# Full-array broadcasts and head sums, and alternating column halves, in the mixer of a hybrid decoder trunk

## The chip, the cores and the metric

The kernel runs on one core of a Trainium2 chip. The metric is device time in microseconds (us); a time before or after is the median of several runs. Beside it one execution is profiled: every instruction has a start and a duration on its engine. PE is TensorE's matmul, PEld its weight load, DVE is VectorE, ACT ScalarE, POOL GpSimd, SP the queue that issues most transfers.

## The reference

Two decoder layers over a sequence of 512 tokens, model width 1024, all in float32. Only the mixer of layer 0 is touched by the change. Its lines, shortened:

```python
hn = rms_norm(h, mix_norm_w[0])
proj = hn @ hyb_w_in[0]                     # [z | xBC | dt | q | k | v]
# A: state space heads, 16 heads of 64, chunks of 128 tokens, state 128
a_cs = cumsum(dt * a_head)                  # per chunk
y_diag = (C B^T * exp(segsum(a))) (x dt)
y_off  = C (carried states) * exp(a_cs)
y_a = gated_group_rms_norm(y_diag + y_off + x * D, z, norm_w)
# B: 16 query heads of 64 on 2 key heads, window of 128 tokens, blocks of 128
q, k = rms_norm(q, q_norm_w), rms_norm(k, k_norm_w)      # over each head's 64 channels
p = softmax with sink (q k^T / 8 + bias, previous and current block)
y_b = p v
h = h + concat(y_a, y_b) @ hyb_w_out[0]
```

After it come a gated MLP, a convolution module and a second gated MLP, which the change leaves alone.

## The kernel before

Activations lie with channels on the 128 partitions and the 512 tokens along the row. A weight matrix is cut into tiles of 128x1024 that SP loads one after the other; `wsplit` cuts each into a high and a low fp32r part (ACT, then DVE), and `gemm` (L131) makes three matmuls of 512 columns for each of the eight inner tiles, at L136, L137 and L138. So one output tile of a projection is 24 matmuls. Products that are not split (transposes, L489, L506, L513, L681) are float32, and the trace has two matmul records for each of them.

The mixer runs through its head pairs j = 0 to 7 (heads j and j + 8 together). The loop at L558 puts out, for each j, a projection tile of x, a tile for queries or keys, and the stages of earlier head pairs: `ssd_states` (L461: transposes L465, two broadcasts L474), `ssd_carry` (L485: L489), `ssd_outputs` (L500: L506, the broadcast of `pair_bcast` at L259, L513). `head_sums` (L524) sums the squares of one query tile over each head for the norm. Then comes attention, `attn_prep` (L619, one `pair_bcast` for each head pair), `attn_logits` (L634) and `attn_values` (L662), in units of (head pair, block of 128 queries), the values three units behind the logits; the gate tiles (L704) are mixed in between. The order on each engine comes from the tile framework's scheduler at build time, outside the stretches of `manual_schedule`; on the chip each engine works through its list in order.

Four kinds of matmul are named below.

- Broadcasts. `rows_t` holds per-head rows (a value and its rounding rest, 32 rows each): partitions 64 to 127 the cumulated decays, partitions 0 to 63 the norm factors of queries and keys. A matmul with a selecting matrix spreads one row over the partitions: L474 for one head, L259 for the two heads of a pair. Both use 64 rows of the array and all 128 columns.
- Head sums at L533, with a selecting matrix of 32 columns, written to 32 partitions of `st_q`; the high part `cv` first, then the low part `th`.
- L506, the product within a chunk: 64 columns for head e = 0 go to partitions 0 to 63 of the bank, those for e = 1 to partitions 64 to 127. Four chunks c for e = 0, then four for e = 1. The operand `ms[0]` comes from DVE and `ms[1]` from POOL (L481).
- L681, the attention values, in the same two column halves: for e = 0 both key blocks b, then for e = 1.

Of the kernel before, what the change touches and what calls it, by code (L numbers as in the profile page):

```python
# [8 lines left out]
F32R = mybir.dt.float32r  # L9
# [5 lines left out]
P = 128  # L15
T = 512
NB = T // P
# [26 lines left out]

CONSTS = {}
_n = 0
for _name, _w in (("ident", P), ("triu", P), ("pairs", 18), ("halves", 73), ("stack", 32)):
    CONSTS[_name] = (_n, _w)
    _n += _w
NCST = _n  # L50
# [10 lines left out]
def kernel(ctx: ExitStack, tc: tile.TileContext, x, w_in, w_dt, w_out,  # L61
                             pw1, pw2, w_up0, w_up1, w_dn0, w_dn1, par, cst, btab, out):
    nc = tc.nc
    V, S, G, TE = nc.vector, nc.scalar, nc.gpsimd, nc.tensor
# [9 lines left out]
    def nm(s):  # L74
        uid[0] += 1
        return f"{s}_{uid[0]}"

    base = {"wr", "wh", "wl", "xr", "nsum", "nsq", "nvar", "nr", "nrb", "cv", "ct", "th"}
    phase = [sb]
# [10 lines left out]
    f32 = lambda ap: ap.bitcast(F32)  # L90
# [11 lines left out]
    def con(name):  # L102
        o, w = CONSTS[name]
        return ctile[:, o : o + w]
# [6 lines left out]
    ident, triu = con("ident"), con("triu")  # L111
# [113 lines left out]
    def mixer(norm, nxt):  # L225
# [21 lines left out]
        def hi_lo_rows(bank, r0):  # L247
            S.copy(rows_t[r0 : r0 + 64], bank[r0 : r0 + 64])
            V.tensor_tensor(rows_t[r0 + 32 : r0 + 64], bank[r0 + 32 : r0 + 64],
                            f32(rows_t[r0 + 32 : r0 + 64]), op=ALU.subtract)  # L250

        def pair_bcast(tag, j, r0):
            sel = phase[0].tile([P, P], F32R, name=nm("sel"), tag="sel", bufs=2)
            a, b = (j, j + 8) if j < 8 else (16, 17)
            rr = slice(r0, r0 + 64)
            for half, q in zip(HALF, (a, b)):
                V.tensor_copy(sel[rr, half], con("pairs")[rr, q : q + 1].to_broadcast([64, 64]))
            bank = bank_of(tag)
            TE.matmul(bank, sel[rr], rows_t[rr], start=True, stop=True)  # L259
            return bank  # L260

        def dt_chain(dts):
# [44 lines left out]
                V.tensor_copy(dst.rearrange("p j c e -> p c e j"), src.rearrange("p (c e j) -> p c e j", c=NB, e=2))  # L307
            return cs, et, dtj, ddj

        # the first tiles of the projection, fed tile by tile as x arrives  # L310
        first, ws, banks = [], [], {}
        with tc.manual_schedule():
            warm = mk([P, 1], "warm")
# [98 lines left out]
                part(2, k)  # L412
        ops, rb, r = norm.ops, norm.rb, norm.r
        pairs = mk([P, 18], "pairs", F32R)
        V.tensor_copy(pairs, con("pairs"))
        halves = mk([P, 73], "halves", F32R)
        V.tensor_copy(halves, con("halves"))
        wqk = mk([P, 1], "wqk")
        V.tensor_scalar(wqk, prm("qw"), prm("kw"), 0.125, op0=ALU.mult, op1=ALU.mult)
# [1 line left out]
        V.tensor_scalar(nsink, prm("sink"), -1.0, None, op0=ALU.mult)  # L421
        chw = mk([P, 60], "chw")
        V.tensor_scalar(chw, prm("scw", 0, 60), 0.5, None, op0=ALU.mult)
        # convolved channels of the state space heads
        def conv_silu(i, dst):
            v = scaled(proj(), rb)
            t = sbt("ct", 2)
# [33 lines left out]
        def ssd_states(j):  # L461
            g = j // 4
            bank = bank_of("pb")
            for c in range(NB):
                TE.transpose(bank[:, blk(c)], xs[j][:, blk(c)], ident)  # L465
            xdt, xdd = (sbt("c", 4) for _ in range(2))
            V.tensor_tensor(v4(xdt), v4(bank), dtj[:, j].unsqueeze(3).to_broadcast([P, NB, 2, 64]), op=ALU.mult)
            G.tensor_tensor(v4(xdd[:, : 3 * P]), v4(xdt[:, : 3 * P]),
                            ddj[:, j, 0:3].unsqueeze(3).to_broadcast([P, 3, 2, 64]), op=ALU.mult)
            ms = []  # L470
            for e in range(2):
                hd = e * 8 + j
                bank = bank_of("pa")
                TE.matmul(bank, pairs[64:P, hd : hd + 1].to_broadcast([64, P]), rows_t[64:P], start=True, stop=True)  # L474
                rl = sbt("a", 4, 514)[:, :T]
                for c in range(NB):
                    S.activation(rl[:, blk(c)], bank[:, blk(c)], AF.Relu, scale=-1.0,
                                 bias=cs[:, c * 16 + hd : c * 16 + hd + 1])
                S.activation(rl, rl, AF.Exp, scale=-1.0)
                mt = sbt("b", 3)  # L480
                (V, G)[e].tensor_tensor(mt, rl, cbm[g], op=ALU.mult)  # L481
                ms.append(mt)
            ssd[j] = [xdt, ms, xdd]
# [16 lines left out]
        def ssd_outputs(j):  # L500
            g = j // 4
            xdt, ms, sm = ssd.pop(j)
            yd = bank_of("pb")
            for e in range(2):
                for c in range(NB):
                    TE.matmul(yd[HALF[e], blk(c)], xdt[:, c * P + e * 64 : c * P + e * 64 + 64], ms[e][:, blk(c)],  # L506
                              start=True, stop=True)
            cb2 = pair_bcast("pa", j, 64)
            ec = sbt("d", 3)
            S.activation(ec[:, P:], cb2[:, P:], AF.Exp)  # L510
            yo = bank_of("pc")
            for c in range(1, NB):
                TE.matmul(yo[:, blk(c)], sm[:, blk(c - 1)], cfm[g][:, blk(c)], start=True, stop=True)  # L513
            V.tensor_tensor(ec[:, P:], yo[:, P:], ec[:, P:], op=ALU.mult)
            V.scalar_tensor_tensor(xs[j], xs[j], prm("sd", j), yd, op0=ALU.mult, op1=ALU.add)
            G.tensor_tensor(xs[j][:, P:], xs[j][:, P:], ec[:, P:], op=ALU.add)

        # keys, values, queries
        kraw = sbt("bc", 4)
        vfm = sbt("bc", 4)  # L520
        qraw = [None] * 8
# [2 lines left out]
        def head_sums(src, n):  # L524
            sq = sbt("nsq", 1)
            S.activation(sq, src, AF.Square)
            hi = sbt("cv", 2, T, F32R)
            V.tensor_copy(hi, sq)
            lo = sbt("th", 1, T, F32R)
            V.tensor_tensor(lo, sq, f32(hi), op=ALU.subtract)  # L530
            w = halves[:, 41:73] if n == 8 else halves[:, 9 - n : 41 - n]
            for i, o in enumerate((hi, lo)):
                TE.matmul(st_q[0:32], w, o, start=n == 8 and i == 0, stop=n == 7 and i == 1)  # L533

        late = []

# [75 lines left out]
            V.tensor_tensor(kla[half], kt[0:64], f32(kha[0:64]), op=ALU.subtract)  # L612
            V.tensor_tensor(klb[half], kt[64:P], f32(khb[64:P]), op=ALU.subtract)

        # attention
        head = {}
        yb = []

# [43 lines left out]
        def attn_values(j, c):  # L662
            lt = soft.pop((j, c))
            if c == 0:
                acc[j] = bank_of("pc")
            yp = acc[j]
            tb = bank_of("pb")
            pt = sbt("b", 3)
            blks = (0, 1) if c else (1,)
            for b in blks:  # L670
                for e in range(2):
                    TE.transpose(tb[:, blk(b * 2 + e)], lt[:, e, blk(b)], ident)  # L672
            o0 = blks[0] * 2 * P
            if c % 2:
                S.copy(pt[:, o0:], tb[:, o0:])
            else:
                V.tensor_copy(pt[:, o0:], tb[:, o0:])
            for e in range(2):
                for b in blks:
                    o = (c - 1 + b) * P + e * 64  # L680
                    TE.matmul(yp[HALF[e], blk(c)], vtok[:, o : o + 64], pt[:, blk(b * 2 + e)],  # L681
                              start=b == blks[0], stop=b == 1)
            if c == NB - 1:
                yh = sbt("att", 16, T, F32R)
                S.copy(yh, yp)
                yl = sbt("att", 16, T, F32R)
                V.tensor_tensor(yl, yp, f32(yh), op=ALU.subtract)
                yb.append((yh, yl))
# [10 lines left out]
            if i >= LAG:  # L699
                attn_values(*units[i - LAG])  # L700

        # gates
        gs = [sbt("bc", 4) for _ in range(2)]
        for j in range(8):  # L704
            v = scaled(proj(), rb)
# [498 lines left out]
def _layout(inputs):  # L1204
# [64 lines left out]
        c[n::32, o["pairs"] + n] = 1  # L1269
    c[:64, o["halves"] + 9] = 1  # L1270
    c[64:, o["halves"] + 17] = 1
    c[:64, o["halves"] + 41 + 16] = 1
    c[64:, o["halves"] + 41 + 17] = 1
    a["cst"] = c

    for n in range(32):
# [27 lines left out]
```

## Time and profile before

| | |
|---|---|
| median of 3 runs | 1336.65 us (1335.57 to 1338.5) |
| profiled execution: span from first to last instruction | 1336.0 us |
| median less span | 0.65 us |
| busy PE, PEld | 97%, 78% of the span |
| busy DVE, ACT, POOL | 66%, 41%, 17% |

The profiled execution is told by its span alone; what lies around the span is taken as the 0.65 us between it and the median. A matmul's duration in the trace holds the run through the array after its last column went in, so durations of neighbours overlap. What one matmul costs the next is read from the distance of their starts.

### The profile page before, as it was taken

To read this page: it belongs to the slowest core of one execution; us is meant where nothing else is said; L and a number is where in the kernel's file an instruction comes from. 1 tells how busy PE (TensorE), PEld (TensorE's weight loads), DVE (VectorE), ACT (ScalarE), POOL (GpSimd) and SP (SyncE) were. 2 spreads that over 40 slices of the span, in tenths; PEclk is the share of its full clock that TensorE was granted. 3 is DMA by queue.
4 is the path that set the end of the run, shared out by engine and by line. 5 is a ranking of instruction groups with operands and counts; after the bars stand their busy time and mean duration, and the time that the engine had idled before them with its cause. 6 is when DMAs were issued, how large, how long until landed. Compare 5 with 4: busy or idle time off the path is not lost.

```text
span 1336.0 us, 17056 instructions
## 1 busy us (share of the span) xinstructions
PE 1298.3 (97%) x6480; PEld 1040.7 (78%) x6480; DVE 884.8 (66%) x1430; ACT 541.3 (41%) x855; POOL 226.5 (17%) x264
## 2 busy tenths in 40 slices
PE   9999999999999999999999999687999999999998
PEld 7877777778888888888888866556888888888887
DVE  6976759985348777777323368897667777774221
ACT  5465537863234333333222244324633433332120
POOL 0031214540210000000000176672500000000000
PEclk9999999999999999999999999889999999999999
DMA  6212212212333333333233273532232233333331
GB/s 214 96 48 63 64 64 64 64 34 78 95 98 95 95 95 97 99 103 89 87 103 88 87 196 109 133 87 91 79 96 96 95 95 95 96 94 106 104 114 38
DMA packets 41553, 125.08 MB, mean 94 GB/s; under 512 B 4864, under 2 KB 7936, under 8 KB 41472
## 3 DMA queue, kind: packets, MB, share of 16 engines
q1 hardware_dynamic: 40752, 123.46, 30.0%
q8 instruction: 51, 0.84, 0.2%
q10 hardware_dynamic: 720, 0.55, 0.2%
q14 instruction: 30, 0.25, 0.1%
HBM read 119.64 MB, written 4.35 MB: 93 GB/s over the span
## 4 chain that ended last, share of the span: by engine, by line
PE 84%; DVE 9%; POOL 3%; ACT 2%; issue 2%; DMA 1%; POOLq 0%; ACTq 0%; DVEq 0%
PE mm L136 24%; PE mm L137 24%; PE mm L138 24%; DVE g L888 3%; POOL yp L903 1%; PE pb L506 1%; PE pc L681 1%; PE pb L672 1%; DVE wl L851 1%; DVE g L961 1%; PE pa L870 1%; PE pa L137 1%; PE pa L138 1%; PE pa L136 1%; PE pc L513 0%
## 5 line engine op out<-in xcount | busy, mean ns | idle before, releaser
L136 PE MATMUL mm<-xr,wh 128*128 128x512 f32 (+1 forms) x1136 | 442.4, 389 | 0.9 <-ACT wh L847 0.9
L138 PE MATMUL mm<-xr,wl 128*128 128x512 f32 (+1 forms) x1136 | 439.3, 387 | 2.7 <-DVE wl L851 2.7
L137 PE MATMUL mm<-xr,wh 128*128 128x512 f32 (+1 forms) x1136 | 439.4, 387 | 0.0
L120 ACT CAST wh<-wr 128x1024 fp32r<-128x1024 f32 (+1 forms) x178 | 183.6, 1032 | 466.0 <-PE mm L137 422.5
L121 DVE TENSOR_TENSOR wl<-wr,wh 128x1024 fp32r<-128x1024 f32 (+1 forms) x178 | 214.4, 1204 | 163.9 <-ACT wh L120 158.8
L136 PEld LDWEIGHTS mm<-xr,wh 128*128 128x128 f32 x1136 | 214.2, 189 | 47.3 <-issue 4.7
L138 PEld LDWEIGHTS mm<-xr,wl 128*128 128x128 f32 x1136 | 214.1, 189 | 46.3 <-DVE wl L851 2.9
L137 PEld LDWEIGHTS mm<-xr,wh 128*128 128x128 f32 x1136 | 214.3, 189 | 42.1 <-issue 0.6
L137 PE MATMUL mm<-g,wh 128*128 128x512 f32 x368 | 145.0, 394 | 0.0
L222 DVE TENSOR_TENSOR cv<-mm,nrb 128x512 f32<-128x512 f32 x114 | 78.2, 689 | 96.4 <-PE mm L138 91.6
L138 PE MATMUL mm<-g,wl 128*128 128x512 f32 x352 | 138.7, 394 | 0.0
L136 PE MATMUL mm<-g,wh 128*128 128x512 f32 x352 | 138.7, 394 | 0.0
L217 DVE SCALAR_TENSOR_TENSOR ct<-cv,par_ffn,ct 128x510 f32<-128x510 f32 (+1 forms) x176 | 131.0, 747 | 3.5 <-issue 0.4
L194 POOL TENSOR_TENSOR nsum<-nsum,nsq 128x512 f32<-128x512 f32 x21 | 34.0, 1617 | 433.0 <-ACT nsq L193 433.0
L137 PEld LDWEIGHTS mm<-g,wh 128*128 128x128 f32 x368 | 68.8, 187 | 17.0
L136 PEld LDWEIGHTS mm<-g,wh 128*128 128x128 f32 x352 | 65.8, 187 | 16.4
L138 PEld LDWEIGHTS mm<-g,wl 128*128 128x128 f32 x352 | 65.8, 187 | 16.2
L214 ACT ACTIVATE ct<-cv,par_ffn 128x512 f32<-128x512 f32 x88 | 71.4, 813 | 3.2 <-DVE cv L222 3.0
L903 POOL TENSOR_TENSOR yp<-yp,pr 128x512 f32<-128x512 f32 x36 | 59.9, 1664 | 37.4 <-ACT pr L902 35.8
L780 ACT ACTIVATE th<-ct 128x512 f32<-128x512 f32 x44 | 27.8, 632 | 84.5 <-DVE ct L217 84.5
L888 DVE SCALAR_TENSOR_TENSOR g<-u,par_conf,g 128x512 f32<-128x512 f32 x42 | 56.2, 1337 | 1.1
L791 DVE TENSOR_TENSOR h<-h,mm 128x512 f32<-128x512 f32 x16 | 11.0, 688 | 59.1 <-PE mm L138 59.1
(344 smaller groups left out, 1519.4 us busy)
## 6 DMA issues: line engine op xcount, KB each, us to landing
wr<-w_up SPq DMA_DIRECT2D x88, 512.0 KB, 3.5
wr<-w_in SPq DMA_DIRECT2D x29, 512.0 KB, 3.6
wr<-w_dn SPq DMA_DIRECT2D x32, 448.0 KB, 3.3
wr<-pw SPq DMA_DIRECT2D x24, 512.0 KB, 3.6
wr<-w_out SPq DMA_DIRECT2D x16, 512.0 KB, 3.6
wr<-w_dn SPq DMA_DIRECT2D x16, 512.0 KB, 3.5
u<-du SPq DMA_DIRECT2D x24, 262.0 KB, 4.7
u<-du SPq DMA_DIRECT2D x16, 140.0 KB, 2.9
```

Source lines behind the costliest of these rows:

```text
L120: S.copy(wh[:, :n], raw[:, :n])
L121: V.tensor_tensor(wl[:, :n], raw[:, :n], f32(wh[:, :n]), op=ALU.subtract)
L136: TE.matmul(bank, wh[:, c], xh, start=first and i == 0, stop=False)
L137: TE.matmul(bank, wh[:, c], xl, start=False, stop=False)
L138: end = TE.matmul(bank, wl[:, c], xh, start=False, stop=last and i == n - 1)
L194: eng.tensor_tensor(self.sum, self.sum, sq, op=ALU.add)
L214: S.activation(t, v, AF.Identity, bias=bias, scale=w(taps - 1))
L217: V.scalar_tensor_tensor(t[:, s:], v[:, : T - s], w(k), t[:, s:], op0=ALU.mult, op1=ALU.add)
L222: V.tensor_tensor(v, bank, rb, op=ALU.mult)
L780: S.activation(sg, c, AF.Silu)
L888: V.scalar_tensor_tensor(y[j], win(j, k), w(j, k), cvp[j, None] if k == ks[0] else y[j], op0=ALU.mult, op1=ALU.add)
L903: G.tensor_tensor(yp[j], yp[j], pr, op=ALU.add)
```

## The change

Broadcasts (L259, L474): the selecting matrices and `rows_t` are used with all 128 rows; the rows that do not belong are zero in the selecting matrix. For this the two `sel` tiles become fixed tiles, and the unused halves of `pairs`, `rows_t` and `sel` are cleared at the start; before the first attention broadcast (j = 8) the upper halves of `sel` are cleared. Head sums (L533): the selecting matrix has 128 columns instead of 32, so the constant table `halves` grows from 73 to 265 columns. L506 and L681: the loops over e and over c (or b) change places, so that matmuls into the two column halves alternate.

```diff
-for _name, _w in (("ident", P), ("triu", P), ("pairs", 18), ("halves", 73), ("stack", 32)):
+for _name, _w in (("ident", P), ("triu", P), ("pairs", 18), ("halves", 265), ("stack", 32)):
...
+        sels = [mk([P, P], f"sel{i}", F32R) for i in range(2)]
+        turn = [0]
+
+        def clear(t):
+            V.memset(f32(t), 0.0)
+            V.tensor_copy(t, f32(t))
+
         def pair_bcast(tag, j, r0):
-            sel = phase[0].tile([P, P], F32R, name=nm("sel"), tag="sel", bufs=2)
+            sel = sels[turn[0] % 2]
+            if j == 8:
+                for t in sels:
+                    clear(t[64:P])
+            turn[0] += 1
...
-            TE.matmul(bank, sel[rr], rows_t[rr], start=True, stop=True)
+            TE.matmul(bank, sel, rows_t, start=True, stop=True)
...
-        V.tensor_copy(pairs, con("pairs"))
-        halves = mk([P, 73], "halves", F32R)
+        clear(pairs[0:64])
+        V.tensor_copy(pairs[64:P], con("pairs")[64:P])
+        clear(rows_t[0:64])
+        for t in sels:
+            clear(t[0:64])
+        halves = mk([P, 265], "halves", F32R)
...
-                TE.matmul(bank, pairs[64:P, hd : hd + 1].to_broadcast([64, P]), rows_t[64:P], start=True, stop=True)
+                TE.matmul(bank, pairs[:, hd : hd + 1].to_broadcast([P, P]), rows_t, start=True, stop=True)
...
-            for e in range(2):
-                for c in range(NB):
+            for c in range(NB):
+                for e in range(2):
                     TE.matmul(yd[HALF[e], blk(c)], xdt[:, c * P + e * 64 : c * P + e * 64 + 64], ms[e][:, blk(c)],
                               start=True, stop=True)
...
-            w = halves[:, 41:73] if n == 8 else halves[:, 9 - n : 41 - n]
+            w = halves[:, 137:265] if n == 8 else halves[:, 9 - n : 137 - n]
             for i, o in enumerate((hi, lo)):
-                TE.matmul(st_q[0:32], w, o, start=n == 8 and i == 0, stop=n == 7 and i == 1)
+                TE.matmul(st_q, w, o, start=n == 8 and i == 0, stop=n == 7 and i == 1)
...
-            for e in range(2):
-                for b in blks:
+            for b in blks:
+                for e in range(2):
                     o = (c - 1 + b) * P + e * 64
                     TE.matmul(yp[HALF[e], blk(c)], vtok[:, o : o + 64], pt[:, blk(b * 2 + e)],
                               start=b == blks[0], stop=b == 1)
```

The order of instructions on TensorE, for the head pair j = 2, as one example of the pairs 2 to 6. Before, in the old line numbers (`halves` marks the head sums, `pb<-b,c` is L506 with `b` for `ms` and `c` for `xdt`, `pa<-rows_t` the broadcasts; the last columns are partitions and columns of the output):

```order
312 L533 MATMUL mm_499<-cv_926,halves 32x512
313 L506 MATMUL pb_932<-b_827,c_815 64x128 x3
314 L533 MATMUL mm_499<-th_928,halves 32x512
315 L506 MATMUL pb_932<-b_827,c_815 64x128
316 L506 MATMUL pb_932<-b_837,c_815 64x128 x4
317 L259 MATMUL pa_944<-rows_t,sel_941 128x512
318 L513 MATMUL pc_948<-bc_424,d_885 128x128 x3
319 L465 MATMUL pb_955<-ctile,xs_839 128x128 x4
320 L474 MATMUL pa_964<-rows_t,pairs 128x512
321 L474 MATMUL pa_974<-rows_t,pairs 128x512
```

The same place of the changed kernel, where L506 has become L521, L533 L548, L259 L270 and L513 L528:

```order
325 L548 MATMUL mm_509<-cv_934,halves 128x512
326 L521 MATMUL pb_940<-b_835,c_823 64x128
327 L521 MATMUL pb_940<-b_845,c_823 64x128
328 L521 MATMUL pb_940<-b_835,c_823 64x128
329 L521 MATMUL pb_940<-b_845,c_823 64x128
330 L548 MATMUL mm_509<-th_936,halves 128x512
331 L521 MATMUL pb_940<-b_835,c_823 64x128
332 L521 MATMUL pb_940<-b_845,c_823 64x128
333 L521 MATMUL pb_940<-b_835,c_823 64x128
334 L521 MATMUL pb_940<-b_845,c_823 64x128
335 L270 MATMUL pa_951<-rows_t,sel_85 128x512
336 L528 MATMUL pc_955<-bc_434,d_893 128x128 x3
```

The low head sum stands between four and four matmuls instead of three and five, and the two operands `b` of the halves take turns; the rest of the list keeps its order.

On TensorE around the head pair j = 1, before:

```order
263 L259 MATMUL pa_799<-rows_t,sel_796 128x512
264 L474 MATMUL pa_819<-rows_t,pairs 128x512
265 L506 MATMUL pb_787<-b_668,c_656 64x128 x4
266 L506 MATMUL pb_787<-b_678,c_656 64x128 x4
267 L489 MATMUL pc_745<-c_657,kv_475 128x128 x3
268 L465 MATMUL pb_810<-ctile,xs_680 128x128 x4
269 L474 MATMUL pa_829<-rows_t,pairs 128x512
```

and in the changed kernel (L480 is the old L465, L489 the old L474, L504 the old L489):

```order
269 L270 MATMUL pa_807<-rows_t,sel_86 128x512
270 L521 MATMUL pb_796<-b_678,c_666 64x128
271 L489 MATMUL pa_827<-rows_t,pairs 128x512
272 L138 MATMUL mm_848<-xr_153,wl_852 128x512
273 L480 MATMUL pb_818<-ctile,xs_690 128x128 x3
274 L521 MATMUL pb_796<-b_688,c_666 64x128
275 L521 MATMUL pb_796<-b_678,c_666 64x128
276 L504 MATMUL pc_754<-c_667,kv_485 128x128 x3
277 L521 MATMUL pb_796<-b_688,c_666 64x128
278 L521 MATMUL pb_796<-b_678,c_666 64x128
279 L521 MATMUL pb_796<-b_688,c_666 64x128
280 L521 MATMUL pb_796<-b_678,c_666 64x128
```

One block of L506 has become three blocks with full-array matmuls between them; at j = 0 one block has become two in the same way.

On POOL in the same stretch, where `c<-c,ddj` is L468, `b<-a,kv` is L481 and `xs` is L516, before:

```order
12 L468 TENSOR_TENSOR c_657<-c_656,ddj 128x384
13 L481 TENSOR_TENSOR b_678<-a_672,kv_482 128x512
14 L516 TENSOR_TENSOR xs_500<-xs_500,d_736 128x384
15 L468 TENSOR_TENSOR c_816<-c_815,ddj 128x384
16 L481 TENSOR_TENSOR b_837<-a_831,kv_482 128x512
17 L516 TENSOR_TENSOR xs_540<-xs_540,d_801 128x384
```

and changed:

```order
12 L483 TENSOR_TENSOR c_667<-c_666,ddj 128x384
13 L496 TENSOR_TENSOR b_688<-a_682,kv_492 128x512
14 L531 TENSOR_TENSOR xs_510<-xs_510,d_745 128x384
15 L496 TENSOR_TENSOR b_845<-a_839,kv_492 128x512
16 L483 TENSOR_TENSOR c_824<-c_823,ddj 128x384
17 L531 TENSOR_TENSOR xs_550<-xs_550,d_809 128x384
```

For j = 2 the product `b` now stands ahead of `c`, on which L489 of that pair waits.

## Rows read from the trace of the kernel before

**Rows 1.** The page: busy time of the engines over the span, and the shares of the engines in the chain that ended last.

```profile
PE 1298.3 (97%) x6480; PEld 1040.7 (78%) x6480; DVE 884.8 (66%) x1430; ACT 541.3 (41%) x855; POOL 226.5 (17%) x264
...
PE 84%; DVE 9%; POOL 3%; ACT 2%; issue 2%; DMA 1%; POOLq 0%; ACTq 0%; DVEq 0%
```

**Rows 2.** Busy time by stage: the stretch in us, its length, then busy us (and instructions) of PE, PEld, DVE, ACT and POOL, the granted clock, the DMA share and GB/s. The first is the state space part, the second attention with the gates.

```profile
60.00:190.00 130.00, 129.33 (x684) 100.21 (x683) 87.72 (x156) 67.49 (x148) 28.34 (x32) 1.00 0.19 59
...
210.00:290.00 80.00, 77.95 (x579) 60.31 (x578) 71.45 (x235) 62.91 (x180) 45.35 (x124) 1.00 0.17 53
```

**Rows 3.** Timeline of PE through the state space work of one head pair: start in us, length of the (merged) row in us, instruction, rows*columns of the array, shape, count.

```profile
93.21 0.39 PE L138 MATMUL mm<-xr,wl 128*128 128x512 f32 x1
93.44 0.40 PE L533 MATMUL mm<-cv,halves 128*32 128x512 f32 x1
93.77 0.87 PE L506 MATMUL pb<-b,c 128*64 128x128 f32 x6
94.56 0.42 PE L533 MATMUL mm<-th,halves 128*32 128x512 f32 x1
94.92 1.09 PE L506 MATMUL pb<-b,c 128*64 128x128 f32 x10
95.94 0.49 PE L259 MATMUL pa<-rows_t,sel 64*128 64x512 f32 x1
96.36 0.94 PE L513 MATMUL pc<-bc,d 128*128 128x128 f32 x6
97.14 0.60 PE L465 MATMUL pb<-ctile,xs 128*128 128x128 f32 x4
97.67 0.72 PE L474 MATMUL pa<-rows_t,pairs 64*128 64x512 f32 x2
98.32 0.50 PE L136 MATMUL mm<-xr,wh 128*128 128x512 f32 x1
98.65 0.40 PE L137 MATMUL mm<-xr,wh 128*128 128x512 f32 x1
```

**Rows 4.** Timeline of PE at three places where matmuls into parts of the columns stand in a row: L506 for j = 0, L681 in attention, and L870 in the later convolution module, which goes through four column quarters in turn.

```profile
75.43 1.58 PE L506 MATMUL pb<-b,c 128*64 128x128 f32 x16
...
224.05 1.15 PE L681 MATMUL pc<-b,bc 128*64 128x128 f32 x16
...
781.06 3.64 PE L870 MATMUL pa<-u,dg 128*32 128x512 f32 x32
```

**Rows 5.** Weight loads: of the head sums at L533 (ns: least, median, most), and from the page those of L137 with 128 columns (busy us, mean ns).

```profile
L533 PEld LDWEIGHTS mm<-th,halves x9: 106/106/108, 94.6 to 189.1; 128*32 128x32 f32 x9
...
L137 PEld LDWEIGHTS mm<-xr,wh 128*128 128x128 f32 x1136 | 214.3, 189 | 42.1 <-issue 0.6
```

**Rows 6.** Timeline of PE around the broadcast of one attention head pair; columns as in rows 3.

```profile
220.65 0.39 PE L642 MATMUL pa<-kv,c 128*128 128x256 f32 x1
220.96 0.49 PE L259 MATMUL pa<-rows_t,sel 64*128 64x512 f32 x1
221.38 1.09 PE L672 MATMUL pb<-ctile,lt 128*128 128x128 f32 x8
222.23 0.48 PE L137 MATMUL mm<-xr,wh 128*128 128x512 f32 x1
...
222.78 0.28 PE L641 MATMUL pa<-kv,c 128*128 128x256 f32 x1
222.90 0.28 PE L642 MATMUL pa<-kv,c 128*128 128x256 f32 x1
```

**Rows 7.** Timeline of PE where four float32 transposes are followed by an fp32r matmul, both on the full array.

```profile
198.36 0.60 PE L600 MATMUL pb<-ctile,bc 128*128 128x128 f32 x4
198.72 0.48 PE L136 MATMUL mm<-xr,wh 128*128 128x512 f32 x1
199.03 0.39 PE L137 MATMUL mm<-xr,wh 128*128 128x512 f32 x1
```

**Rows 8.** Timelines of PE, DVE and POOL at the next head pair: start, length, instruction, shapes, count, and in brackets the idle time before it and what ended it.

```profile
110.05 0.40 PE L533 MATMUL mm<-cv,halves 128*32 128x512 f32 x1
...
111.18 0.43 PE L533 MATMUL mm<-th,halves 128*32 128x512 f32 x1
...
110.12 0.69 DVE L530 TENSOR_TENSOR th<-nsq,cv 128x512 fp32r<-128x512 f32 x1
...
101.63 1.29 POOL L481 TENSOR_TENSOR b<-a,kv 128x512 f32<-128x512 f32 x1 [1.79 <-ACT a L479]
```

**Rows 9.** The chain of work that ended last, in order of time, at the end of attention and behind it: start, us, what.

```profile
284.84 0.49 PE pb L672 x3
...
285.89 0.64 ACT th L707
...
298.47 1.13 PE pb L164 x8
```

**Rows 10.** Busy time by stretch behind attention; columns as in rows 2.

```profile
296.50:298.40 1.90, 0.01 (x1) 0.00 (x0) 1.69 (x8) 0.64 (x1) 0.62 (x1) 1.00 0.00 0
...
299.70:306.50 6.80, 6.80 (x21) 5.54 (x21) 5.57 (x13) 3.00 (x5) 0.00 (x0) 0.50 0.26 77
```

**Rows 11.** Timeline of DVE at the start of the kernel.

```profile
0.91 0.48 DVE L341 MEMSET att<- 128x512 f32 x1 [0.91 <-PEq L1296]
...
5.24 0.23 DVE L343 CAST att<-att 128x128 fp32r<-128x128 f32 x1 [3.39 <-DMA att<-w_dt]
```

More of the change, by code (lines that the diff above doesn't have):

```diff
@@ L1271, in _layout @@
     c[64:, o["halves"] + 17] = 1
-    c[:64, o["halves"] + 41 + 16] = 1
-    c[64:, o["halves"] + 41 + 17] = 1
+    c[:64, o["halves"] + 137 + 16] = 1
+    c[64:, o["halves"] + 137 + 17] = 1
     a["cst"] = c
```

## The prediction

> **What bounds the kernel now.** I first read the busy shares and the chain by engine: TensorE is busy 97% of the span and holds 84% of the chain [rows 1], so work taken from TensorE shortens the kernel unless another engine stands close behind. Then the stages: in the state space part (60 to 190 us) PE is busy 129.3 of 130 us while DVE has 87.7 and ACT 67.5; in attention with the gates (210 to 290) PE has 77.95 of 80, but DVE 71.45 [rows 2]. The first stage is TensorE's alone, the second nearly DVE's too. Last the timeline of PE, by starts and not by durations. The reader is to see that full-array fp32r matmuls of 512 columns start 0.23 us apart (93.21 to 93.44, and the whole projections likewise) and float32 records of 128 columns 0.11 us apart (six L513 and four L465), and that every step between the full array and a part of it costs more than that [rows 3].
>
> **What a step costs.** In rows 3, against these two distances:
> - Out of a part: L259 with 64 rows, to L513: 0.42 instead of 0.23. It holds an entry (it follows L506 with 64 columns) and an exit, 0.19 together.
> - The six L513 after it take 0.78 (96.36 to 97.14) instead of 0.67: 0.10 for the entry into the full array.
> - Four L465 take 0.53 instead of 0.44: 0.09 for the exit to L474. The two L474 take 0.65 instead of 0.45: entry and exit, 0.20. The L136 behind them takes 0.33: entry, 0.10.
> So an exit costs 0.09 to 0.10, an entry about 0.10, and about 0.05 where 64 columns are entered. It is not the change between float32 and fp32r: four L600 and one L136, both full, take 0.67 (198.36 to 199.03), just 4 x 0.11 + 0.23 [rows 7]. And it does not hold for the 32 columns of the head sums: the L138 ahead of `cv` keeps its 0.23 [rows 3].
>
> **What alternation is worth.** The same 16 records of 64 columns take 1.58 us at L506 and 1.15 at L681 [rows 4]. At L681 the other half comes after two matmuls (four records), and 1.15 is eight steps of 0.11 and a tail of a quarter us: all records run in twos. At L506 it comes after four matmuls (eight records), and 1.58 is four steps more: 12, so only the middle overlaps. L870 takes its four quarters in turn. One of its records has four times the columns of those, so a step is 0.43, and 32 records are through in 3.64 us [rows 4], eight steps and a tail: turns do overlap. L681 is overlapped already; its new order gains nothing that I can see, and I count 0.
>
> **State space part, part by part.** One head pair, j = 2 to 6, from `cv` at 93.44 to L137 at 98.65, 5.21 us [rows 3]. After, in order:
> - `cv` 0.33 (0.23 and the exit to L506), as now.
> - Four L506, eight records in four steps: 0.05 + 0.44 + 0.09 = 0.58 (now six records, 0.79).
> - `th` between two such blocks: 0.10 + 0.23 + 0.10 = 0.43. Now 0.36. This edit costs: its weights load in 106 ns with 32 columns and in about 189 with 128 [rows 5], and behind an exit nothing hides the 0.08.
> - Four L506 again 0.58 (now ten records, 1.02).
> - L259 0.33, L513 0.67, L465 0.44, two L474 0.45, L136 0.23: no step among them.
> Sum 4.04, so 1.17 less, five times: 5.85. For j = 7 no head sum stands inside: L506 0.43, L259 0.09, L513 0.10: 0.6. For j = 0 and 1 the blocks are cut into two and three. Three more blocks cost an entry and an exit on either side, about 0.3 each, 0.9 together; four steps of overlap (0.4) and the broadcasts among them bring about as much, and I count 0. For two pairs of broadcasts ahead of them I count 0.4 each, as in rows 3 (0.09, 0.20 and 0.10): 0.8. The stage gives 7.25.
>
> What lies beside it. POOL's `ms[1]` is ready at 102.9, seven us before L506 of that pair at 110.4 [rows 8], so the first alternating pair does not wait. The low head sum is the tight one: DVE ends `th` at 110.81, PE takes it at 111.18, 1.13 after `cv` [rows 8]. After, `th` comes 0.91 behind `cv` (0.33 + 0.58), so 0.15 of the margin of 0.37 is left, and nothing waits; were DVE later, each of the five pairs would lose what it is late. At j = 2 POOL makes `b` ahead of `c`, 1.29 us [rows 8] that L489 may wait for; its cost lies between 0 and 1.3, and since `c` now ends well ahead I take 0.2. The eight clears on DVE at the start stand ahead of a wait of 3.39 us for a transfer [rows 11]; two are of 512 columns, at most the 0.48 us of the 128x512 memset each, and six are of 128 or fewer: an estimate of 2 us, hidden. Without that cover the first matmuls would be late by what exceeds 3.39. The later clears (64x128) run where DVE is idle a third of the time [rows 2]. The larger constant table adds 96 KB to one transfer, 1.7 us even at the 59 GB/s of rows 2; weights are loaded up to three tiles ahead, and a tile is 24 matmuls of 0.23, 5.4 us: 0. The stage: 7.0.
>
> **Attention.** One broadcast: L642 0.31 (220.65 to 220.96) with an entry behind L681 and an exit, after it 0.12 + 0.10 = 0.22 (0.12 from 222.78 to 222.90); L259 0.42, after it 0.23; eight L672 0.85 (221.38 to 222.23), of them 0.05 entry [rows 6]. That is 0.33, nine times with the key's: 3.0 of TensorE's time. Between 0 and 3.0 arrives, because DVE is busy 89% here [rows 2]. The end of attention is handed from PE's last transposes (284.84) to ACT at 285.89 and from there to DVE until L164 at 298.47 [rows 9]; PE idles 1.9 us ahead of it [rows 10]. What reaches 284.84 earlier arrives; what PE gains behind it does not. Chain pieces up to there are mostly PE's, so I take 1.8.
>
> Sum 8.8. The profiled execution's 1336.0 becomes 1327.2; with the 0.65 between span and median, 1327.85, about 1327.8.
>
> **A rule that speaks against the change.** The two L474 of a pair hold 0.65 (97.67 to 98.32) [rows 3], so these two 64-row matmuls do not run side by side. The Trainium skill (TensorEngine Tiling (Array Packing), When to Use Tiling) recommends two row tiles for a contraction of up to 64, each with its own matmul in parallel. By it the broadcasts should stay at 64 rows and be paired, and 0.23 for each of eight pairs, 1.8 us, would be given up here. The rows show no such pairing before, since both matmuls take the same rows, so the sum gives nothing up.
>
> **Rivals.**
> 1. DVE, ACT and POOL take over. For: 71.45 of 80 us in attention, and the tail on DVE. Against: PE is the chain's main engine until 284.84. Attention gives 0, and 1.5 of the lead is waited away: 1336.65 - 7.0 + 1.5 = 1331.2.
> 2. Everything arrives and a stretch at half clock falls away. Behind the idle 1.9 us PE ran 6.8 us at a granted clock of 0.50, the 1.2 GHz level [rows 10]; at the full level that work takes 3.4. 1336.65 - 7.25 - 3.0 - 3.4 = 1323.0. Against: PE will idle ahead of L164 as before.
> 3. The 64 rows are not what the steps cost, so broadcasts gain nothing and only alternation does (2.17 for L506 and `th` becomes 1.59): 5 x 0.58 + 0.43 = 3.3, 1333.3. Against: the steps of rows 3 and 6 stand exactly at the 64-row matmuls.
> 4. Slower: halves that take turns do not overlap, because the next weights for the other half are not loaded beside a running matmul. L506 loses the overlap it has, four steps in the three undivided blocks and two in the five divided ones, 22 x 0.11 = 2.4, and L681 all of its own: 14 matmuls a pair, two records each, eight pairs, in 224 steps instead of 112, 12.3. Less 3.5 and 3.0 for broadcasts and `th`: 8.2 more, 1344.8. It decides if 16 records take 1.75 us. For it: L681 now has two matmuls of one half in a row, not one. Against: L870's turns [rows 4]. The Trainium skill (TensorE: Matmul & The Clock Gate, Part 3, The mechanism) says that weight loads overlap matmuls in flight only where the row group differs, and here both halves have all rows; by this rule the rival holds. The trace disagrees already: whole projections, all on one row group, load 189 ns beside matmuls 0.23 apart.
>
> **Chances.** Forecast 0.70 (own range 1325.5 to 1330.5: attention's 0 to 3.0, and about 1 us that the three runs of before differ by), rival 1 0.16, rival 2 0.06, rival 3 0.05, rival 4 0.03. The range 1322.5 to 1332.5 leaves out rivals 3 and 4, 0.08, and about as much at the edges of the others. A measurement of this kernel can tell 0.2% (2.7 us) from no change, so faster means under 1334.0: forecast, 1, 2 and most of 3, less a little for what I do not see: 0.93 faster, 0.04 same, 0.03 slower.
>
> **What would show it.** From one `cv` to the next, 16.61 us now (93.44 to 110.05) [rows 3, 8], 15.4 after. A block of eight L506 records in 0.6 to 0.75 us with its tail. L259 to its successor 0.33 in the state space part and 0.23 in attention; L474 to L474 0.23; `th` 0.43. L681 rows of 16 still 1.15. PE idle ahead of L164 no shorter than 1.9. I am wrong if head sums wait for DVE each time, if L506 takes 1.5 us or more, or if the stage before 190 us shrinks by less than 6.

## The result and the profile after

The changed kernel takes 1327.68 us (median of 4 runs, 1326.15 to 1328.72) beside 1337.55 us for the kernel before on the same chip (4 runs, 1335.57 to 1338.5): a ratio of 0.9928, with a 95% interval of 0.9914 to 0.9942. The forecast was 1327.8. In the code after the change the lines have moved: L506 is now L521, L259 L270, L474 L489, L489 L504, L513 L528, L465 L480, L533 L548, L672 L687, L681 L696, and L641 and L642 are L656 and L657.

The page of the kernel after, for [rows 1]: busy times of the engines.

```profile
PE 1288.5 (97%) x6480; PEld 1037.3 (78%) x6480; DVE 884.8 (67%) x1442; ACT 541.0 (41%) x855; POOL 226.8 (17%) x264
```

PE has 9.8 us less, the span 9.1 (1336.0 to 1326.9); the count of matmuls is the same. The twelve instructions more are the clears on DVE.

Timeline of PE after the change, through the state space work of the same head pair as in [rows 3], columns as there.

```profile
92.56 0.40 PE L548 MATMUL mm<-cv,halves 128*128 128x512 f32 x1
92.89 0.66 PE L521 MATMUL pb<-b,c 128*64 128x128 f32 x8
93.48 0.50 PE L548 MATMUL mm<-th,halves 128*128 128x512 f32 x1
93.91 0.66 PE L521 MATMUL pb<-b,c 128*64 128x128 f32 x8
94.50 0.50 PE L270 MATMUL pa<-rows_t,sel 128*128 128x512 f32 x1
94.83 0.83 PE L528 MATMUL pc<-bc,d 128*128 128x128 f32 x6
95.50 0.60 PE L480 MATMUL pb<-ctile,xs 128*128 128x128 f32 x4
95.85 0.71 PE L489 MATMUL pa<-rows_t,pairs 128*128 128x512 f32 x2
96.40 0.39 PE L136 MATMUL mm<-xr,wh 128*128 128x512 f32 x1
96.63 0.39 PE L137 MATMUL mm<-xr,wh 128*128 128x512 f32 x1
```

From `cv` to the second projection matmul behind the pair it is 4.07 us (92.56 to 96.63), where the sum of starts gave 4.04 and the kernel before took 5.21. Term by term: eight L521 records 0.59 (0.58 expected), `th` 0.43 (0.43), the broadcast at L270 0.33 (0.33), six L528 0.67 (0.67), four L480 0.35 and two L489 with them 0.90 (0.89). The next `cv` starts at 107.99, 15.43 later (15.4 expected, 16.61 before).

Behind attention, for [rows 9, 10]: PE's timeline after the change (the bracket is the idle time before the row and what ended it), and then a window of 6.8 us (columns as in rows 2).

```profile
289.33 1.13 PE L164 MATMUL pb<-ctile,gr 128*128 128x128 f32 x8 [1.96 <-DVE gr L742]
290.30 1.46 PE L158 MATMUL pb<-ones,bc 128*128 128x1 f32 x8
```

```profile
290.60:297.40 6.80, 6.80 (x20) 5.54 (x21) 5.57 (x13) 2.96 (x5) 0.00 (x0) 0.50 0.24 77
```

The tail on DVE, PE's idle time ahead of L164 and the 6.8 us at a granted clock of 0.50 are all as before, only 9.1 us earlier.

**How gains are located below.** The traces reach the first L164 between 27.82 and 29.19 us, and the edits do not explain it: the kernels of experiments 5, 6, 7 and 9, which start like the changed kernel, reach it at 28.07 to 28.77, the changed kernel at 28.98. So a gain is counted from the first L164, which PE's timelines before and after show at 29.19 and 28.98 us, 0.21 that belongs to the start:

```profile
29.19 1.05 PE L164 MATMUL pb<-ctile,nr 128*128 128x128 f32 x8
```

```profile
28.98 1.05 PE L164 MATMUL pb<-ctile,nr 128*128 128x128 f32 x8
```

The last L681 starts at 286.57 before, its successor L696 at 277.42 after: 9.15, less 0.21 is a lead of 8.94 us. Other leads are worked out from starts in the same way, each from one execution. The changed kernel and that of experiment 9 have the same order on PE up to there, and their leads differ by 0.10 (8.94 and 8.84); so much is noise.

| kernel (profiled span, us) | lead at the last head sum | behind attention | at the end |
|---|---|---|---|
| after (1326.9) | 7.19 | 8.94 | 8.93 |
| broadcasts only (1328.2) | 4.45 | 6.17 | 6.71 |
| alternation only (1331.7) | 3.04 | 3.43 | 3.41 |
| head sums only (1336.1) | -0.51 | -0.63 | -0.59 |
| after, head sums on 32 columns (1325.4) | 7.53 | 9.27 | 9.31 |
| after, L696 in the old order (1326.2) | 7.20 | 8.78 | 8.77 |
| after, L521 in twos (1326.6) | 6.96 | 8.70 | 8.85 |
| after, attention's broadcasts on 64 rows (1326.1) | 7.18 | 7.45 | 9.56 |
| after, head sums on 32 columns and late (1324.5) | 8.84 | 10.66 | 10.79 |

Where the broadcasts alone gain another 0.5 at the end, they do so in the convolution module, where nothing was edited: the lead is 6.16 at the L164 at 756 us and 6.71 at that at 972. The cause was not followed.

### The profile page after: what moved, and what is told of

The parts are those of the page before. It is cut to its first block, busy times and chain, and to the rows that moved or that the text cites. A ratio compares the mean times of both kernels' runs of the same rounds, so it can differ in the third digit from the quotient of the medians.

```text
span 1326.9 us, 17068 instructions
## 1 busy us (share of the span) xinstructions
PE 1288.5 (97%) x6480; PEld 1037.3 (78%) x6480; DVE 884.8 (67%) x1442; ACT 541.0 (41%) x855; POOL 226.8 (17%) x264
## 4 chain that ended last, share of the span: by engine, by line
PE 69%; DVE 8%; POOL 2%; issue 1%; ACT 1%; POOLq 0%; ACTq 0%; DVEq 0%
PE mm L136 21%; PE mm L137 21%; PE mm L138 21%; DVE g L903 3%; POOL yp L918 1%; DVE wl L866 1%; DVE g L976 1%; PE pa L885 1%; PE pc L696 1%; PE pa L137 1%; PE pa L138 1%; PE pa L136 1%; PE pb L687 0%; POOL g L922 0%; PE mm L1036 0%
## 5 line engine op out<-in xcount | busy, mean ns | idle before, releaser
L136 PE MATMUL mm<-xr,wh 128*128 128x512 f32 (+1 forms) x1136 | 442.0, 389 | 1.0 <-ACT wh L862 1.0
L137 PE MATMUL mm<-xr,wh 128*128 128x512 f32 (+1 forms) x1136 | 439.7, 387 | 0.0
L136 PEld LDWEIGHTS mm<-xr,wh 128*128 128x128 f32 x1136 | 214.6, 189 | 45.9 <-issue 2.8
L137 PEld LDWEIGHTS mm<-xr,wh 128*128 128x128 f32 x1136 | 214.7, 189 | 41.7 <-DVE xr L184 0.4
L137 PE MATMUL mm<-g,wh 128*128 128x512 f32 x368 | 145.0, 394 | 0.0
L136 PE MATMUL mm<-g,wh 128*128 128x512 f32 x352 | 138.7, 394 | 0.0
L137 PEld LDWEIGHTS mm<-g,wh 128*128 128x128 f32 x368 | 68.8, 187 | 17.1
L136 PEld LDWEIGHTS mm<-g,wh 128*128 128x128 f32 x352 | 65.8, 187 | 16.3
```

What stands on the lines that cost most here:

```text
L136: TE.matmul(bank, wh[:, c], xh, start=first and i == 0, stop=False)
L137: TE.matmul(bank, wh[:, c], xl, start=False, stop=False)
```

## The experiments

**1. The broadcasts alone.** The head sums go back to 32 columns, the loops at L521 and L696 to the old order.

```diff
-            for c in range(NB):
-                for e in range(2):
+            for e in range(2):
+                for c in range(NB):
                     TE.matmul(yd[HALF[e], blk(c)], xdt[...], ms[e][:, blk(c)], ...
...
-                TE.matmul(st_q, w, o, ...
+                TE.matmul(st_q[0:32], w, o, ...
```

> The broadcasts use all rows; head sums keep 32 columns and both loops keep their old order. Theory (each step between the full array and 64 rows costs about 0.1 us out and 0.1 us in): per head pair 2 to 6 of the state space part 0.59 us less, so cv to cv 16.0 us; at the end of that part 4.7 us ahead of the kernel before, at the end of attention 6.5 ahead, and the time 0.49% below before. Rival (the steps belong to something else than the 64 rows): cv to cv stays 16.6 and the time does not move.

Measured: 1330.09 us (4 runs) beside 1336.53 (12 runs of the kernel before), ratio 0.9954 [0.9937, 0.997]. PE's timeline:

```profile
91.01 0.40 PE L548 MATMUL mm<-cv,halves 128*32 128x512 f32 x1
...
92.49 1.09 PE L521 MATMUL pb<-b,c 128*64 128x128 f32 x10
93.51 0.50 PE L270 MATMUL pa<-rows_t,sel 128*128 128x512 f32 x1
93.85 0.83 PE L528 MATMUL pc<-bc,d 128*128 128x128 f32 x6
94.51 0.60 PE L480 MATMUL pb<-ctile,xs 128*128 128x128 f32 x4
94.87 0.70 PE L489 MATMUL pa<-rows_t,pairs 128*128 128x512 f32 x2
95.41 0.39 PE L136 MATMUL mm<-xr,wh 128*128 128x512 f32 x1
95.64 0.40 PE L137 MATMUL mm<-xr,wh 128*128 128x512 f32 x1
```

With the old order of L521, its ten records keep their 1.02. L270 falls from 0.42 to 0.34, L528 from 0.78 to 0.66, L480 from 0.53 to 0.36, the two L489 from 0.65 to 0.54, and L136 from 0.33 to 0.23: each step that stood at a 64-row matmul goes with it, and the 0.11 left at L270 belongs to the change back from L521's 64 columns. From `cv` to `cv` it is 16.0, as expected; the leads of 4.45 and 6.17 are 0.3 under the 4.7 and 6.5 expected. The rival in which the 64 rows cost nothing is refuted.

**2. The alternation alone.** The kernel before, with the two loops exchanged at L506 and at L681.

```diff
-            for e in range(2):
-                for c in range(NB):
+            for c in range(NB):
+                for e in range(2):
...
-            for e in range(2):
-                for b in blks:
+            for b in blks:
+                for e in range(2):
```

> Only the two loops over halves change places. Theory (halves that take turns run in twos, where the old order left four or six steps of 0.11 us alone): cv to cv 16.0 us, 0.58 less for head pairs 2 to 6 and 0.4 for pair 7; pairs 0 and 1 lose up to 0.5 because their blocks are cut into pieces; 2.8 us less at the end of the state space part, nothing more in attention, 0.2% below before. Rival (turns do not overlap): 16 records of attention values take 1.75 us instead of 1.15, and the kernel is 14 us slower.

Measured: 1333.49 us (9 runs) beside 1336.53, ratio 0.9977 [0.9967, 0.9987]. PE's timeline:

```profile
93.15 0.40 PE L533 MATMUL mm<-cv,halves 128*32 128x512 f32 x1
93.48 0.66 PE L506 MATMUL pb<-b,c 128*64 128x128 f32 x8
94.06 0.42 PE L533 MATMUL mm<-th,halves 128*32 128x512 f32 x1
94.41 0.66 PE L506 MATMUL pb<-b,c 128*64 128x128 f32 x8
95.00 0.50 PE L259 MATMUL pa<-rows_t,sel 64*128 64x512 f32 x1
95.43 0.94 PE L513 MATMUL pc<-bc,d 128*128 128x128 f32 x6
```

Two blocks of eight take 0.58 and 0.59, where six and ten took 0.79 and 1.02; `th` 0.35 and L259 0.43 are as before. Turns overlap; the rival that ended slower is refuted. In attention the order of L681 brings 0.39, which the forecast had put at nothing. The pairs j = 0 and 1 lose, because their blocks are now cut: the lead is -0.66 at the `cv` of j = 2 (93.15 here, 93.44 before), and -0.01 at that pair's L259, when its own two blocks have made the loss good.

**3. The head sums alone.** The kernel before with 128 columns at L533.

```diff
-            w = halves[:, 41:73] if n == 8 else halves[:, 9 - n : 41 - n]
+            w = halves[:, 137:265] if n == 8 else halves[:, 9 - n : 137 - n]
...
-                TE.matmul(st_q[0:32], w, o, ...
+                TE.matmul(st_q, w, o, ...
```

> Only the head sums are widened from 32 to 128 columns. Theory (32 columns cost no step against the full array, and behind an exit the wider weight load shows): th takes 0.43 us instead of 0.36 in five head pairs, 0.4 us slower in all, too little for the time to tell. Rival (32 columns are a part of the array like 64 rows): the 32-column matmuls lose two steps of 0.1 us beside full matmuls, and the kernel gains up to 1 us.

One run: 1337.91 us, and a lead of -0.59 at the end. From `cv` to `cv` a pair takes 16.69, 0.1 more, all of it at `th`: 0.43 to 0.44 to its successor instead of 0.34 to 0.36. This part of the change costs, as the forecast had it. The three parts add up: 4.45 + 3.04 - 0.51 = 6.98 at the last head sum (after: 7.19), 6.17 + 3.43 - 0.63 = 8.97 behind attention (8.94).

**4. After, with the head sums back on 32 columns.** The last lines of experiment 1's diff, alone.

> The change without the wider head sums (32 columns kept). Theory: cv to cv 15.4 us as in the changed kernel less 0.08, so 15.35; 0.4 us faster than the changed kernel, 0.75% below before. Rival (the wider head sums bring part of the gain): cv to cv 15.6 or more, and the time above the changed kernel's.

Measured: 1327.17 us (4 runs) beside 1336.53, ratio 0.9931 [0.9916, 0.9946]. The interval does not part it from the changed kernel; the lead does, 9.27 behind attention against 8.94, and `cv` to `cv`, 15.34 against 15.43. In PE's timeline `th` takes 0.34 to its successor, not 0.43:

```profile
92.36 0.42 PE L548 MATMUL mm<-th,halves 128*32 128x512 f32 x1
92.70 0.66 PE L521 MATMUL pb<-b,c 128*64 128x128 f32 x8
```

**5. After, with the old order at L696 alone.**

```diff
-            for b in blks:
-                for e in range(2):
+            for e in range(2):
+                for b in blks:
                     o = (c - 1 + b) * P + e * 64
```

> The change, but the attention values keep their old order (both key blocks of a half, then the other half). Leads over the kernel before are counted from the norm's broadcast at 29 us, since the first 10 us differ from run to run. Theory, formed after the run with alternation alone: in blocks of 12 and 16 records the old order loses half a step, 0.05 us, and of the change's 1.7 us in attention about 0.35 is from the new order: blocks of 16 records again take 1.07 us to the next start instead of 1.02, and the lead behind attention is 8.55 instead of 8.9. Rival (the prediction's count of nothing): 8.9 as in the changed kernel.

One run: 1327.96 us (before: 1336.99); lead behind attention 8.78 instead of 8.94, where 8.55 was expected and 8.9 by the rival. The first two rows are this kernel's, the other two the changed one's, each pair a block of twelve and its successor on PE:

```profile
211.46 0.93 PE L696 MATMUL pc<-b,bc 128*64 128x128 f32 x12
212.32 0.39 PE L657 MATMUL pa<-kv,c 128*128 128x256 f32 x1
```

```profile
212.35 0.88 PE L696 MATMUL pc<-b,bc 128*64 128x128 f32 x12
213.16 0.38 PE L657 MATMUL pa<-kv,c 128*128 128x256 f32 x1
```

Twelve records take 0.86 in the old order and 0.81 in the new one, sixteen 1.07 and 1.02 (260.68 to 261.70 after), eight 0.59 in both. So the old order loses half a step, 0.05, in ten of the eleven longer blocks and 0.02 in the other, 0.5 in all. Where alternation stood alone 0.39 of it arrives; here it is 0.16, little above the noise of 0.1; where the rest stays is not shown.

**6. After, with L521's halves changing every two matmuls** instead of every one.

```diff
-            for c in range(NB):
-                for e in range(2):
+            for c0, e, c in [(c0, e, c0 + d) for c0 in (0, 2) for e in range(2) for d in range(2)]:
+                if True:
```

> The change, but in the product within a chunk each half has two matmuls in a row (chunks 0 and 1 of e = 0, then of e = 1, then chunks 2 and 3) instead of one. Theory (records of the other half are taken ahead as far as four records away): the blocks of eight records stay at 0.59 us and cv to cv at 15.4. Rival (only strict turns overlap): the blocks take 0.8 us or more and cv to cv is at least 15.8.

One run: 1328.39 us (before: 1336.99); lead 6.96 at the last head sum. A block of eight in twos, PE's timeline:

```profile
92.63 0.67 PE L521 MATMUL pb<-b,c 128*64 128x128 f32 x8
93.23 0.50 PE L548 MATMUL mm<-th,halves 128*128 128x512 f32 x1
```

0.60, against 0.59 in strict turns, and `cv` to `cv` 15.44. It is enough that the other half comes within four records; that it came after eight made L506 slow. The first two records start 0.02 apart (92.63 and 92.65) although the list has four of one half first, so TensorE takes records of the other half ahead of the list.

**7. After, with attention's nine broadcasts on 64 rows.** Where r0 is 0 the matmul takes 64 rows as before.

```diff
+            if r0:
+                TE.matmul(bank, sel, rows_t, ...)
+            else:
+                TE.matmul(bank, sel[rr], rows_t[rr], ...)
-            TE.matmul(bank, sel, rows_t, ...)
```

> The change, but the nine broadcasts of attention use 64 rows again. Theory (TensorE sets the pace in attention, and steps there are worth most of what they take): lead from the norm's broadcast 7.2 at the end of the state space part as in the changed kernel, and 7.5 behind attention, so that the broadcasts there bring 1.4 of the 3.0 us that they hold. Rival (DVE sets the pace): 8.5 or more behind attention without them.

One run: 1327.84 us (before: 1336.99), lead 7.45 behind attention. So the nine broadcasts bring 8.94 - 7.45 = 1.49 of the 3.0 that PE holds. Where the rest stays, the changed kernel's timeline shows, first PE, where the broadcast is at L270, then POOL:

```profile
222.40 0.40 PE L270 MATMUL pa<-rows_t,sel 128*128 128x512 f32 x1
222.64 1.03 PE L687 MATMUL pb<-ctile,lt 128*128 128x128 f32 x8
223.43 0.48 PE L137 MATMUL mm<-xr,wh 128*128 128x512 f32 x1
...
240.19 0.39 PE L270 MATMUL pa<-rows_t,sel 128*128 128x512 f32 x1
240.42 1.55 PE L687 MATMUL pb<-ctile,lt 128*128 128x128 f32 x8
241.73 0.48 PE L136 MATMUL mm<-xr,wh 128*128 128x512 f32 x1
```

```profile
240.07 1.30 POOL L671 TENSOR_SCALAR lt<-lt,rec 128x256 f32<-128x256 f32 x2 [0.88 <-DVE rec L669]
```

L270 to L687 takes 0.23 to 0.24 in both places, where L259 to L672 took 0.42. But the eight transposes at 240.42 take 1.31 to their successor, against 0.79 at 222.64: the sixth starts at 241.43, behind the `lt` that POOL scales until 241.37, and POOL itself waited for `rec` from DVE. PE comes earlier, and meets the softmax. From one broadcast to the next the lead grows by 0.00, 0.11, 0.37, 0.44, 0.04 and 0.12, then by 0.22 and 0.37: by 0.44 from the one at 222.40, by 0.12 from that at 240.19. In the stretch that brings nothing, the first, PE's wait for DVE's `c` at L656 (L641) has grown from 0.2 to 0.4.

This kernel's end lead of 9.56 is no gain of the edit: it grows by 1.58 between the first L164 behind attention and the second, and by another 0.5 in the convolution module, as that of the broadcasts alone. Behind the same idle 1.96 us ahead of L164, its half-clock stretch lasted 3.4 us (292.8 to 296.2) and not 6.8, as its window shows, with a mean granted clock of 0.78:

```profile
292.30:300.00 7.70, 7.70 (x28) 6.15 (x29) 5.57 (x13) 3.20 (x6) 0.00 (x0) 0.78 0.22 68
```

**8. After, with the head sums on 32 columns and behind the pair's other work.**

```diff
                 key_query(n)
-                if len(late) > 1:
-                    head_sums(*late.pop(0))
             for fn, j in todo:
                 fn(j)
+            if kind == "q" and len(late) > 1:
+                head_sums(*late.pop(0))
```

> The change with 32-column head sums that are moved behind the stages of the head pair, so that the product within a chunk is one block of 16 records and no head sum stands inside it. Theory (each entry into and exit from the halves costs 0.05 and 0.1, and the head sum inside costs what it takes to leave and re-enter): cv to cv 15.05 instead of 15.35 with 32 columns, 1.4 us ahead of that kernel over five pairs, 0.85% below before. Rival (with the blocks joined something else ends last: DVE's low part, or the products of POOL): cv to cv stays at 15.3 or more.

Measured: 1326.34 us (5 runs) beside 1336.99 (9 runs), ratio 0.9922 [0.9908, 0.9936]; lead 10.66 behind attention. The interval overlaps the changed kernel's; the lead is what parts them. PE's timeline of a pair:

```profile
107.24 1.09 PE L521 MATMUL pb<-b,c 128*64 128x128 f32 x16
108.26 0.50 PE L270 MATMUL pa<-rows_t,sel 128*128 128x512 f32 x1
...
110.17 0.40 PE L548 MATMUL mm<-cv,halves 128*32 128x512 f32 x1
110.40 0.40 PE L548 MATMUL mm<-th,halves 128*32 128x512 f32 x1
110.63 0.40 PE L136 MATMUL mm<-xr,wh 128*128 128x512 f32 x1
```

Nothing cuts the sixteen records (1.02), and both sums stand among full-array matmuls at 0.23 each. What the wide head sum was meant to make cheaper, a matmul between two blocks of 64 columns, is better moved out: from `cv` to `cv` 15.1 (15.05 expected) instead of 15.43, of which the 32 columns by themselves bring 0.09 (experiment 4).

**9 and 10. Work for PE in its idle time ahead of L164.** To the changed kernel, and to that of experiment 8, ten 128x128 matmuls are added behind the sum of squares; nothing reads their output.

```diff
+            if g == 0:
+                spare = bank_of("pc")
+                for i in range(10):
+                    TE.matmul(spare[:, :P], var[:, i % NB : i % NB + 1].to_broadcast([P, P]), ident, start=True, stop=True)
```

> The change, with ten extra 128x128 matmuls into a spare bank, whose output nobody reads, put into TensorE's idle 1.9 us ahead of the first L164 behind attention; they hold 2.2 us. Theory (the stretch of 6.8 us at a granted clock of 0.50 behind that idle follows from it, and the work in it takes 3.4 us at the full level): no granted clock under 1.00 between 285 and 300 us, the lead over the kernel before grows from 8.9 to about 12 between the first and the second L164 there, and the time falls by 3 us, to 0.95% below before. Rival (the low clock comes from the one-column sums L158 or is there by chance): the stretch at 0.50 stays, and the time stays at the changed kernel's or 0.3 us above.

> The same ten extra matmuls in the kernel with late 32-column head sums. Theory: both gains add up, lead 10.7 at the first L164 behind attention and about 14 at the second, 1.05% below before. Rival: as for the run before, 0.8% below before, as with late head sums alone.

Measured: 1328.61 us (4 runs, 1326.4 to 1329.79), ratio 0.9939 [0.9925, 0.9953], and 1325.11 us (5 runs, 1324.98 to 1327.73), ratio 0.9923 [0.9909, 0.9936], both beside 1336.99 (9 runs). PE's timeline of the first, and a window of it:

```profile
284.48 2.50 PE L743 MATMUL pc<-ctile,nvar 128*128 128x128 f32 x20 [0.48 <-DVE nvar L739]
286.73 0.47 PE L138 MATMUL mm<-att,wl 128*128 128x512 f32 x1
288.41 1.16 PE L164 MATMUL pb<-ctile,gr 128*128 128x128 f32 x8 [1.21 <-DVE gr L746]
289.41 0.95 PE L158 MATMUL pb<-ones,bc 128*128 128x1 f32 x8
```

```profile
290.00:297.40 7.40, 7.40 (x35) 6.03 (x35) 6.96 (x15) 3.53 (x6) 0.00 (x0) 1.00 0.22 62
```

The idle time is cut into 0.48 and 1.21, and the granted clock stays at 1.00: where the changed kernel ran at the 1.2 GHz level for 6.8 us, this one runs at 2.4, with the one-column sums L158 still there. In experiment 10 the clock is 1.00 there too; in the ten other kernels the stretch stands in every profile, 3.4 or 6.8 us long. So it came from the one idle time of 1.96, and not from L158; whether the length of that idle time counts or the work put into it is not shown. At the second L164 the lead is 12.62 and 14.36, as expected, 3.7 above the kernel without the ten, but by the next, 89 us later, 2.8 of it are gone again. PE's rows say why. The ten matmuls (20 records, 2.25 us) take the place of projection matmuls: 15 of them stand between L158 and the first L164, against 25 after the change, and 19 instead of 7 follow the second L164 before that module's last group. Twelve matmuls of 0.23 are those 2.8. About 0.9 remains in the profiled executions (9.85 against 8.91 at that L164, and 11.60 against 10.71 over experiment 8), and the medians do not show it: the runs of one kernel lie 2.6 to 3.6 us apart. The 0.95% and 1.05% expected of the time did not come (0.61% and 0.77%), because the expectation took the ten matmuls as free. Of all kernels run, that of experiment 8, with or without the ten, has the lowest medians.

## Why the prediction was right

The mechanism held, and the forecast lay 0.1 us from the median, so near by luck. The sum said 8.8 us less; the profiled spans differ by 9.1 and the medians by 9.9, since the median of the kernel before is 1337.55 with a fourth run, and not 1336.65. Nor is the 0.65 that was added what lies around a span: every run on record with a known span took 1.7 to 2.2 us more than it (the changed kernel's profiled one 1328.72, with a span of 1326.9). Taken with such a difference, an estimate, the profiled execution of the kernel before took about 1338 us, and the forecast for it would have been about 1329. By its own steps:

- *Steps of 0.1 out of and into a part of the array, 1.17 a pair.* Right. The lead at the broadcast grows by 1.19, 1.16, 1.16, 1.17 and 1.08 from one pair to the next; experiment 1 alone gives 0.57 to 0.61, and experiment 2 0.63 to 0.66 with 0.48 in the last pair.
- *A head sum on 128 columns costs 0.08.* Right: 0.09 to 0.1 a pair, 0.51 at the last head sum.
- *0.8 for the broadcasts ahead; j = 0 and 1, cut blocks against overlap and broadcasts, 0.* Right within 0.2. The lead at the first L521 is 0.75. From there to the first `cv` the broadcasts alone bring 0.58 (experiment 1) and the alternation alone costs 0.66 (experiment 2); in the changed kernel it falls by 0.08, to 0.67, and without the 0.26 that POOL's order takes (next point) it would rise by 0.18.
- *The state space part, 7.0.* It brought 7.19: 0.67 up to the first `cv` (0.6 by the sum), 5.85 in the five pairs (5.85) and 0.69 for j = 7 (0.6). That includes POOL's order at j = 2, put at 0.2: L504 starts 0.49 after its predecessor, not 0.23, so 0.26, and POOL's `c` ends at 86.26.

```profile
85.82 0.40 PE L138 MATMUL mm<-xr,wl 128*128 128x512 f32 x1
86.31 0.94 PE L504 MATMUL pc<-c,kv 128*128 128x128 f32 x6
```

```profile
84.05 1.42 POOL L496 TENSOR_TENSOR b<-a,kv 128x512 f32<-128x512 f32 x1 [3.67 <-ACT a L494]
85.43 0.83 POOL L483 TENSOR_TENSOR c<-c,ddj 128x384 f32<-128x384 f32 x1
```

- *`th` is tight but in time.* Right. DVE starts it at 92.50 and needs 0.69; PE takes it at 93.48, 0.29 later, and the block ahead of it has its 0.59. In the other four pairs 0.14 to 0.17 is left, the 0.15 of the forecast.
- *Attention, 1.8 of 3.0.* It brought 1.75, but put together otherwise: 1.49 from the broadcasts, 0.16 from the order of L696 and 0.10 that the runs do not assign. The term *"L681 is overlapped already; its new order gains nothing that I can see, and I count 0"* was too small, by 0.05 in each of ten blocks; that rows of 16 would keep their 1.15 failed with it, they have 1.09. And what holds the rest are POOL's `lt` in the middle of the transposes and DVE's `c` ahead of them, which the forecast had named only in general as DVE's 89%.
- *PE's idle time ahead of L164 stays.* Right: 1.96, and the 6.8 us at half clock with it.

Of the rivals, DVE, ACT and POOL took over in part: half of attention's 3.0, nothing of the lead that PE had brought there. The rival in which everything arrives failed at the same place, and at the half-clock stretch; experiments 9 and 10 show that the half-clock stretch can fall away when PE has work there, and that this work costs most of what it gives back. The rule of the Trainium skill on which the slower rival rested (TensorE: Matmul & The Clock Gate, Part 3, The mechanism: weight loads overlap matmuls in flight only where the row group differs) does not hold here: both halves use all rows, and eight records, each with a weight load of 0.13 to 0.14 us of its own, are through in 0.59.

## What to carry to other kernels

On an engine that is never idle, read starts and not durations: what a matmul costs is its distance to the next start, and an odd distance beside a matmul of another tile shape is the price of changing the shape. A lone 64-row matmul among full-array ones is better padded with zero rows; float32 matmuls that fill column halves should change halves at least every two matmuls and stand in one uncut block, with other shapes moved out of it. Time freed on one engine arrives only up to the next hand-over: follow the lead from landmark to landmark, and look where it stops growing.

## What the runs showed of the hardware

- A change between the full array and 64 rows or 64 columns, either way, cost 0.09 to 0.11 us at the last matmul before it and 0.05 to 0.12 at the first one behind it, 0.05 where that one has 64 columns (in the changed kernel `th` takes 0.43 between two blocks of L521, a projection matmul 0.23 to its next); a 32-column fp32r head sum between full-array matmuls cost nothing of the kind (experiment 8: 0.23 to the next start). The Trainium skill (TensorEngine Tiling (Array Packing), Key Properties) says that a change of tiling mode drains TensorE, which the first agrees with and the second does not.
- Behind one and the same idle time of 1.96 us the granted clock stayed at 0.50 for 6.8 us in the changed kernel and for 3.4 us in experiment 7, which is 1.6 us of difference at the second L164 that no edit made.
